# Another order of bank pairs, with accumulating transfers, in the last five stages of a hybrid trunk kernel on one Trainium2 core

## The chip, the core and the metric

One core of one Trainium2 chip runs the whole kernel. The core has a matrix engine (TensorE, "PE" in the profile), a vector engine (VectorE, "DVE"), a scalar engine (ScalarE, "ACT"), a general engine (GpSimd, "POOL") and a queue engine (SyncE, "SP"). TensorE writes its sums into PSUM banks; VectorE and ScalarE read them out. All other data lies in SBUF, and DMA transfers carry it to and from device memory. Each engine works through its own list of instructions in order, and semaphores tie the lists together. The metric is the time of one execution on the device, in microseconds (us); lower is better.

## What is computed

One layer of a streaming model, for a prompt of 1024 rows and eight samples of 16 rows, 1152 rows in all, which the kernel takes as one width of 1152 (two halves of 576, each of two pieces of 288):

```python
h = rms_norm(x, norm_g) * (1 + scale) + shift          # from c @ w_ada
z = h @ w_in    # attention q | k | v | gate | SSD gate | SSD x/B/C | dt | two merge gates
a = (attention over a band of chunks, gated) @ w_att_proj
s = (SSD scan of x/B/C, gated, group norm)   @ w_ssd_proj
y = (sigmoid(g_a) * a + sigmoid(g_s) * s) @ w_out
out = x + mod_gate * y
```

All matrices of 1024 columns that stand at the end (merge gates, attention projection, SSD projection over 2048 rows, output projection) are multiplied as float32 values split into a high and a low fp16 part, with three of the four partial products.

## The kernel before

**The last five stages.** After attention and the SSD scan the program has five dense stages: the merge gates (their last four pairs; eight plain ones go before), the attention projection (`att_dense`), the first half of the SSD projection (`ssd_dense(0)`), its second half (`ssd_dense(1)`) and the output projection (`out_dense`). Each stage has four "quads", 20 in all. A quad computes two column blocks (o = 0, 1) of 128 for both halves (t = 0, 1) of the width, by a scheme of Winograd's kind: seven products in place of eight, on sums and differences of operand blocks and of weight blocks. One product is 24 matmuls of 128x288: four blocks of the inner dimension, two PSUM banks (the two pieces of 288), three fp16 terms (lines 854, 855, 856).

**Banks.** A product goes to a pair of PSUM banks. The pool `s` has one pair of banks; the pools `g` and `d` have three single banks each. In `quad_dense` a pair is two banks of one pool, and the names are `fore` (from `s` in one quad, from `d` in the next), `side` (from `g`) and `lone` (from `s` or `d`, whichever `fore` isn't). Products 0, 5, 6 and 3 are summed one onto the other in `fore`, products 4 and 2 in `side`, product 1 stands alone in `lone`; between two products of one pair the running sum must be read out. The order of a quad is 0, 4, 5, 1, 6, 2, 3. The first quad of each stage (`wide`) interleaves products 0, 4 and 1 by inner block, because its operands are still being made, and reads `fore` out once more before product 3 (`u3`), which then has a pair of its own.

**Reading out.** `kept` copies a pair by ScalarE (line 873, two instructions of 288 columns) or, in the second SSD half, adds it by VectorE onto the first half's result, called the base (line 869). `joined` adds a pair by VectorE onto a copy that was kept (line 879). Product 3's sum goes straight to the stage's own last step (lines 2293, 2309, 2325 by stage).

**Operands.** The right side of a stage is cut into pieces by `pieces`: ScalarE and VectorE make a high part (`halved`, lines 2173 and 2175) and a low part, and differences (lines 2184 to 2187). For the attention projection they come from `att_d`, for the SSD projection from `y_d` times a row of token scales `yb` (lines 2250, 2256, 2261), for the output projection from the merged result below. Line 686 (ScalarE) squares pieces for a running check of magnitudes. Weights are loaded 512 KB at a time (`in_quad_dram`), and split by lines 694 (ScalarE) and 695 (VectorE).

**The merge.** `att_dense` multiplies its result by its gate (line 2293) and stores it in device memory as `att_o` (line 2296, issued by POOL, 16 stores of 128x576). `ssd_dense(0)` stores `acc_d` (lines 2309, 2310). `ssd_dense(1)` loads `acc_d`, the gates and `att_o` again (tiles `acc`, `gs`, `att` of 128x1152, by SP), adds the products onto `acc`, multiplies by the gate (line 2329, 128x576) and adds that onto the `att` tile by VectorE (line 2330, 128x576, 16 times). The `att` tiles, two for each pair, then go through `pieces` into the output projection.

**What sets the order.** Python generators emit the work of each stage in program order (`run`), with `urgent` and `paced` side jobs that give way to each other by an estimated clock: `pause(t)` holds a job until t ns of that clock have gone by, `stored` gives a buffer back 9000 ns after its store. SBUF buffers come from an arena (`walloc`, `alloc`); a job that finds no room waits. Then the class `Order` sorts the instructions of each engine anew: a list scheduler with a cost and a margin for each engine (`SAFE`) and a reach of `AHEAD` instructions. Its result is the order of the queues; what an instruction waits for on the chip is still set by semaphores. `token_sums` (line 1364) sums squares over the columns by three matmuls, after `pause(4500)`; `mod_gate` makes the gate of the output from `c` (matmuls on lines 1077 and 1083, ScalarE on 2357) beside the attention projection. After the last quad a check of all magnitudes (`verdict`, lines 2379 to 2393) decides whether a general kernel must run in place of this one.

## Time and profile before

| | |
|---|---|
| median of three runs | 1721.31 us (1721.12 to 1727.28) |
| the profiled execution | 1722.93 us, span 1721.0 us |
| TensorE matmul | busy 1677.3 us (97%) |
| VectorE | busy 1378.6 us (80%) |
| ScalarE | busy 1061.5 us (62%) |
| POOL | busy 391.5 us (23%) |
| the five stages | from about 1275 us to the end, 20 quads |

The span is the time from the first instruction to the last on the core; the execution's own time is 1.9 us longer. TensorE's matmuls are pipelined: one is shown as 0.28 us long, while they start 0.12 us apart, so that "busy" doesn't mean that none can be put in. The number in square brackets in a timeline is how long the engine was idle just before that instruction, with what ended it.

### The profile page before, as it was taken

Reading aid. Unit: us, or ns where it says so; the run is one execution under the profiler, and the core shown is the slowest. Engines: PE = TensorE matmul, PEld = TensorE weight load, DVE = VectorE, ACT = ScalarE, POOL = GpSimd, SP = SyncE. Lnnn points to the kernel's source line nnn. Section 1 sums busy time; section 2 is a strip of 40 time slices with the busy share of each in tenths; the row PEclk is TensorE's granted clock in tenths of the full one; section 3 lists DMA queues with packets and bytes.
Section 4 is the critical chain, followed back from the end, with each engine's and each line's share of the span. In section 5 each row is a group of like instructions: output and inputs, shape, how many; then the busy total and the mean of one; then the engine's idle time right before and its main releaser. Section 6 shows DMA issues by size and latency. Waiting matters only on the chain.

```text
span 1721.0 us, 36673 instructions
## 1 busy us (share of the span) xinstructions
PE 1677.3 (97%) x14265; PEld 1122.4 (65%) x14265; DVE 1378.6 (80%) x2546; ACT 1061.5 (62%) x2130; POOL 391.5 (23%) x640
## 2 busy tenths in 40 slices
PE   7999999999999999999999999999999999999998
PEld 3556565556565556666666666666667677777776
DVE  6458767878777888989988989996898487878963
ACT  8766556566565567456655756666388575775550
POOL 0134233135133101322321333242231011110000
PEclk9999999999999999999999999999999999999999
DMA  9248789797988688686858767878658786777651
GB/s 383 83 120 212 169 227 228 169 230 189 210 227 189 168 190 228 184 220 199 196 182 271 231 184 242 238 217 272 226 166 294 266 292 207 254 284 259 221 194 58
DMA packets 299105, 369.16 MB, mean 214 GB/s; under 512 B 211676, under 2 KB 213096, under 8 KB 298920
## 3 DMA queue, kind: packets, MB, share of 16 engines
q1 hardware_dynamic: 281896, 307.65, 63.7%
q0 software_dynamic: 17024, 59.06, 9.4%
q8 instruction: 114, 1.87, 0.5%
q14 instruction: 71, 0.58, 0.1%
HBM read 244.08 MB, written 74.06 MB: 185 GB/s over the span
## 4 chain that ended last, share of the span: by engine, by line
PE 51%; DVE 18%; DMA 11%; ACT 11%; issue 7%; POOL 1%; SPq 1%; DVEq 0%; ACTq 0%; POOLq 0%
PE d L945 6%; PE d L948 6%; PE d L946 6%; PE d L998 5%; PE d L1000 5%; PE d L999 5%; ACT arena L686 3%; PE g L1604 2%; DVE arena L2175 2%; DMA arena<-in_quad_dram 2%; DMA arena<-acs_d 2%; DVE arena L695 2%; DVE arena L1802 2%; ACT arena L1988 1%; DMA arena<-sum_d 1%
## 5 line engine op out<-in xcount | busy, mean ns | idle before, releaser
L945 PE MATMUL d<-arena 128*128 128x384 f16 x1320 | 431.0, 327 | 1.4 <-ACT arena L1779 1.4
L948 PE MATMUL d<-arena 128*128 128x384 f16 x1320 | 430.3, 326 | 0.6 <-DVE arena L695 0.6
L946 PE MATMUL d<-arena 128*128 128x384 f16 x1320 | 430.3, 326 | 0.0
L686 ACT ACTIVATE arena<-arena 128x1024 bf16<-128x1024 f32 (+4 forms) x217 | 199.3, 918 | 141.9 <-DMA arena<-in_wall_dram 96.4
L695 DVE SCALAR_TENSOR_TENSOR arena<-arena 128x1024 f16<-128x1024 f32 (+2 forms) x157 | 181.7, 1165 | 42.4 <-ACT arena L694 42.2
L694 ACT ACTIVATE arena<-arena 128x1024 f16<-128x1024 f32 (+2 forms) x157 | 155.1, 994 | 66.5 <-DMA arena<-sum_d 33.1
L945 PEld LDWEIGHTS <-arena 128*128 128x128 f16 x1320 | 129.2, 98 | 90.2 <-issue 13.3
L998 PE MATMUL d<-arena 128*128 128x384 f16 (+1 forms) x568 | 186.8, 329 | 0.0
L1000 PE MATMUL d<-arena 128*128 128x384 f16 (+1 forms) x568 | 186.1, 328 | 0.0
L999 PE MATMUL d<-arena 128*128 128x384 f16 (+1 forms) x568 | 186.1, 328 | 0.0
L948 PEld LDWEIGHTS <-arena 128*128 128x128 f16 x1320 | 129.1, 98 | 86.3 <-DVE arena L695 1.0
L946 PEld LDWEIGHTS <-arena 128*128 128x128 f16 x1320 | 129.2, 98 | 78.5 <-issue 1.6
L1544 ACT ACTIVATE arena<-arena 128x640 f32<-128x640 f32 (+4 forms) x144 | 100.8, 701 | 63.5 <-DVE arena L1547 63.1
L855 PEld LDWEIGHTS <-arena 128*128 128x128 f16 x1120 | 109.7, 98 | 43.9 <-issue 16.3
L854 PE MATMUL d<-arena 128*128 128x288 f16 x440 | 126.3, 287 | 3.7 <-ACT arena L873 3.2
L856 PEld LDWEIGHTS <-arena 128*128 128x128 f16 x1120 | 109.8, 98 | 30.5 <-issue 2.7
L854 PEld LDWEIGHTS <-arena 128*128 128x128 f16 x1120 | 110.0, 98 | 29.5 <-issue 1.7
L855 PE MATMUL d<-arena 128*128 128x288 f16 x440 | 126.2, 287 | 1.1 <-DVE arena L2175 1.1
L856 PE MATMUL d<-arena 128*128 128x288 f16 x440 | 126.1, 287 | 0.0
L854 PE MATMUL s<-arena 128*128 128x288 f16 x360 | 102.9, 286 | 6.5 <-ACT arena L873 3.9
L1802 DVE SCALAR_TENSOR_TENSOR arena<-arena 128x1176 f32<-128x1176 f32 x72 | 103.2, 1434 | 5.5 <-ACT arena L1799 3.8
L2175 DVE SCALAR_TENSOR_TENSOR arena<-arena 128x1152 f16<-128x1152 f32 (+1 forms) x72 | 87.4, 1219 | 21.9 <-ACT arena L2173 21.7
(278 smaller groups left out, 3565.0 us busy)
## 6 DMA issues: line engine op xcount, KB each, us to landing
arena<-in_quad_dram SPq DMA_DIRECT2D x80, 512.0 KB, 5.7
arena<-in_wall_dram SPq DMA_DIRECT2D x77, 512.0 KB, 5.2
sum_d<-arena POOLq DMA_DIRECT2D x40, 512.0 KB, 4.7
arena<-sum_d SPq DMA_DIRECT2D x40, 512.0 KB, 4.8
arena<-acs_d SPq DMA_DIRECT2D x32, 576.0 KB, 5.8
arena<-in_kc_dram SPq DMA_DIRECT2D x64, 256.0 KB, 4.6
arena<-in_vc_dram SPq DMA_DIRECT2D x64, 256.0 KB, 2.9
arena<-in_wada_dram SPq DMA_DIRECT2D x24, 512.0 KB, 10.2
```

The costliest lines, as they stand in the source:

```text
L686: keep(nc.scalar.activation(junk[:, :n], x, AF.Square, scale=scale * n ** -0.5, accum_out=sums[:, c:c + 1]))
L694: keep(nc.scalar.activation(hi, x, AF.Copy, scale=scale))
L695: keep(nc.vector.scalar_tensor_tensor(lo, x, scale, hi, ALU.mult, ALU.subtract))
L854: nc.tensor.matmul(ps, wh, xh[:, c], start=first and k == 0, stop=False, skip_group_check=not first)
L855: nc.tensor.matmul(ps, wh, xl[:, c], start=False, stop=False, skip_group_check=not first)
L856: nc.tensor.matmul(ps, wl, xh[:, c], start=False, stop=k == 3, skip_group_check=not first)
L945: nc.tensor.matmul(ps, hi.r[:, wc], kh.r[:, tok], start=k == 0, stop=False)
L946: nc.tensor.matmul(ps, hi.r[:, wc], kl.r[:, tok], start=False, stop=False)
L948: nc.tensor.matmul(ps, lo.r[:, wc], kh.r[:, tok], start=False, stop=k == nk - 1)
L998: nc.tensor.matmul(ps, kh.r[:, tok], wh, start=k == 0, stop=False)
L999: nc.tensor.matmul(ps, kh.r[:, tok], wl, start=False, stop=False)
L1000: nc.tensor.matmul(ps, kl.r[:, tok], wh, start=False, stop=k == KT - 1)
```

## The change

1. **Order of products.** A quad now runs 0, 4, then product 3 of the quad before (`rest`, held in `pending` and emitted by `flush`), 5, 1, 2, 6. In a `wide` quad the product held over is emitted after the first inner block. `lone` is a fourth pair made of one bank of pool `d` and one of pool `g`. The extra read-out of `fore` in wide quads (`u3`) is gone.
2. **Quick read-outs.** Instructions that read PSUM in these stages are marked; `Order` puts them 300 places ahead and plans a margin of 200 ns for them.
3. **Weights.** The buffers of split weights are taken part by part and given back after the product that uses them last (`w_used`); splitting can go up to two quads ahead (`w_next`).
4. **The merge.** For three of the four pairs in the second SSD half, `att_o` is added by 12 accumulating transfers from device memory into the `acc` tile in SBUF (line 2364 of the new kernel, issued by POOL, 128x576 each). The 12 VectorE adds and six of the eight loads of `att_o` are gone; the pieces of these pairs come from `acc`, after a `pause(9000)`. The last pair still loads `att_o` (`att_last`) and adds by VectorE.
5. **Side jobs.** Loads of the merge tiles follow each half of a pair, `token_sums` pauses for 12000, and `mod_gate` runs at the start of the gates stage.

```diff
+    FAST = 300
+    SAFE_FAST = 200.0
...
+            u["fast"] = u["ins"][0].name in self.fast
+            u["at"] = u["i"] + self.FILL * (u["ins"][0].name in self.fill) - self.FAST * u["fast"]
...
-                    m = self.SAFE_DMA if v["dma"] else self.SAFE[u["eng"]]
+                    m = self.SAFE_DMA if v["dma"] else self.SAFE_FAST if u["fast"] else self.SAFE[u["eng"]]
...
+    pending = []
+
+    def flush():
+        while pending:
+            yield from pending.pop()()
+
+    def quick(x):
+        fast.add(x.ins.name)
+        return x
...
-            return [psd.tile([P, HC], F32, tag="d", name=nm("d")) for _ in range(2)]
-
-        fore = bank(2 if odd else 0)
-        side = bank(1)
+            if n == 2:
+                return [psd.tile([P, HC], F32, tag="d", name=nm("d")) for _ in range(2)]
+            return [psd.tile([P, HC], F32, tag="d", name=nm("d")), pg(HC)]
...
+                if k == 0:
+                    yield from flush()
             begun.update((0, 4, 1))
         yield from product(0, fore)
         p1 = yield from kept(fore, 0, 0)
         yield from product(4, side)
         p5 = yield from kept(side, 1, 1)
+        yield from flush()
+        w_next(i)
         yield from product(5, fore, first=False)
+        w_used(i, 3, 4)
         u2 = yield from kept(fore, 0, 1)
         w_next(i)
-        if not wide:
-            lone = bank(0 if odd else 2)
+        lone = lone or bank(3)
         yield from product(1, lone)
+        w_used(i, 0, 1)
         yield from joined(0, 0, p1, lone)
         w_next(i)
-        if wide:
-            yield from product(2, side, first=False)
+        yield from product(2, side, first=False)
+        yield from joined(0, 1, u2, side)
         yield from product(6, fore, first=False)
...
-        if wide:
-            lone = bank(0 if odd else 2)
-            yield from product(3, lone)
-            yield from joined(1, 0, u3, lone)
-        else:
+        def rest():
             yield from product(3, fore, first=False)
+            w_used(i, 2)
             yield from evict(1, 0, [(g * HC, HC, ps) for g, ps in enumerate(fore)], None) or ()
-        w_done(i)
+
+        pending.append(rest)
...
-                yield from pause(4500)
+                yield from pause(12000)
...
-                m = yield from taken("att", c + o)
+                m = a if c < 6 else (yield from taken("att", o))
...
-                nc.vector.tensor_tensor(m.ap[:, tok], m.ap[:, tok], a.ap[:, tok], ALU.add)
+                if c < 6:
+                    nc.gpsimd.dma_start(a.ap[:, tok], att_o[c + o][:, tok], accum_op=ALU.add)
+                else:
+                    nc.vector.tensor_tensor(m.ap[:, tok], m.ap[:, tok], a.ap[:, tok], ALU.add)
...
-                        urgent.append(pieces(tiles["att"][c], m, out_ops, 0.5 * SM / (SA * SW)))
+                        def last(c=c, m=m):
+                            if c < 6:
+                                yield from pause(9000)
+                            yield from pieces(tiles["acc"][c] if c < 6 else tiles["att"][0], m, out_ops, 0.5 * SM / (SA * SW))
+                        urgent.append(last())
...
-        yield from ready(lambda: len(att_ops) >= 1)
+        yield from ready(lambda: ssd_all[NPAIR])
...
-    items.append((att_dense(), [tile_loads(4, ("ga", gate_d, 0)), ssd_prep(), mod_gate()], [], 0.5))
+    items.append((gates_dense(), [mod_gate(), h_pieces(), att_prep()], [], 0.5))
+    items.append((att_dense(), [tile_loads(4, ("ga", gate_d, 0)), ssd_prep()], [], 0.5))
```

**How it moves instructions.** The first place is VectorE's list in the second quad of the second SSD half. Before, `d_17644`, `d_17645` are the `fore` banks, `g_17646`, `g_17647` the `side` banks, and `s_17749` the `lone` pair:

```order
L869 TENSOR_TENSOR arena<-arena,d_17644 128x288
L869 TENSOR_TENSOR arena<-arena,d_17645 128x288
L879 TENSOR_TENSOR arena<-arena,s_17749 128x288 x2
L879 TENSOR_TENSOR arena<-arena,g_17646 128x288
L2175 SCALAR_TENSOR_TENSOR arena<-arena 128x1152
L2329 SCALAR_TENSOR_TENSOR arena<-arena 128x576
L879 TENSOR_TENSOR arena<-arena,g_17647 128x288
L2330 TENSOR_TENSOR arena<-arena 128x576
L879 TENSOR_TENSOR arena<-arena,d_17644 128x288
L879 TENSOR_TENSOR arena<-arena,d_17645 128x288
L2329 SCALAR_TENSOR_TENSOR arena<-arena 128x576 x2
L2330 TENSOR_TENSOR arena<-arena 128x576 x2
```

In the new kernel the same stretch reads as follows; `d_17602`, `d_17603` are the `fore` banks, `g_17604`, `g_17605` the `side` banks, `d_17722` with `g_17723` the fourth pair, and L901, L2362, L2200 and L2211 are the lines that were L879, L2329, L2175 and L2186:

```order
L901 TENSOR_TENSOR arena<-arena,d_17722 128x288
L901 TENSOR_TENSOR arena<-arena,g_17723 128x288
L698 SCALAR_TENSOR_TENSOR arena<-arena 128x512
L2362 SCALAR_TENSOR_TENSOR arena<-arena 128x576
L901 TENSOR_TENSOR arena<-arena,g_17604 128x288
L901 TENSOR_TENSOR arena<-arena,g_17605 128x288
L2362 SCALAR_TENSOR_TENSOR arena<-arena 128x576
L2200 SCALAR_TENSOR_TENSOR arena<-arena 128x1152
L901 TENSOR_TENSOR arena<-arena,d_17602 128x288
L901 TENSOR_TENSOR arena<-arena,d_17603 128x288
L2211 SCALAR_TENSOR_TENSOR arena<-arena 128x576
L2362 SCALAR_TENSOR_TENSOR arena<-arena 128x576
```

The adds L2330 that followed each gate multiplication are gone from the list, and the two read-outs of a pair stand side by side.

The second place is the end of POOL's list; before:

```order
L2152 DMA gate_d<-arena 128x576 x16
L2296 DMA att_o<-arena 128x576 x16
L2310 DMA acc_d<-arena 128x576 x16
L4159 TENSOR_LOAD again
L4160 COMPARE_AND_BRANCH
```

and in the new kernel:

```order
L2177 DMA gate_d<-arena 128x576 x15
L2329 DMA att_o<-arena 128x576 x16
L2343 DMA acc_d<-arena 128x576 x16
L2364 DMA arena<-att_o 128x576 x12
L4201 TENSOR_LOAD again
L4202 COMPARE_AND_BRANCH
```

The 12 accumulating transfers come behind all stores of POOL's queue, and only the final load of the check's answer comes behind them.

The third place is ScalarE's list ahead of the first quad of the gates, whose banks `s_14627`, `g_14628`, `g_14629` it reads out; before:

```order
L1894 ACTIVATE arena<-d_14594 128x384
L686 ACTIVATE arena<-arena 128x576
L2173 ACTIVATE arena<-arena 128x1152
L686 ACTIVATE arena<-arena 128x576 x3
L694 ACTIVATE arena<-arena 128x1024
L2173 ACTIVATE arena<-arena 128x1152
L686 ACTIVATE arena<-arena 128x1024
L873 ACTIVATE arena<-s_14627 128x288 x2
L873 ACTIVATE arena<-g_14628 128x288
L873 ACTIVATE arena<-g_14629 128x288
```

and in the new kernel, where the banks are `s_14646`, `g_14647`, `g_14648`, and L1919, L689, L697, L2198, L895 are the lines that were L1894, L686, L694, L2173, L873:

```order
L1919 ACTIVATE arena<-d_14601 128x384
L689 ACTIVATE arena<-arena 128x576 x2
L2397 ACTIVATE arena<-g_14629 128x512
L1391 ACTIVATE arena<-g_14656 96x384
L697 ACTIVATE arena<-arena 128x1024
L689 ACTIVATE arena<-arena 128x576 x2
L2198 ACTIVATE arena<-arena 128x1152
L689 ACTIVATE arena<-arena 128x576 x2
L697 ACTIVATE arena<-arena 128x512
L2198 ACTIVATE arena<-arena 128x1152
L895 ACTIVATE arena<-s_14646 128x288 x2
L895 ACTIVATE arena<-g_14647 128x288
```

The read-out of the output gate's matmuls (L2397, from `mod_gate`) and of the token sums (L1391) now stand ahead of this quad's first read-outs.

116 lines of the change are left out of this document (65 added, 51 removed).

## The prediction

> **What bounds the kernel now.** First the page, for the share of each engine and the matrix engine's clock over the span:
>
> ```profile
> span 1721.0 us, 36673 instructions
> PE 1677.3 (97%) x14265; PEld 1122.4 (65%) x14265; DVE 1378.6 (80%) x2546; ACT 1061.5 (62%) x2130; POOL 391.5 (23%) x640
> ```
>
> TensorE bounds the kernel, and no matmul is taken away. What a change of this kind can win is TensorE's stalls. So the second view is what TensorE waited for, over the stretch of the quads (1270 to 1721):
>
> ```profile
> PE s L854 <- ACT arena L873: 3.9, 3, 2.3
> PE d L854 <- ACT arena L873: 3.2, 3, 1.7
> PE g L854 <- ACT arena L873: 2.4, 1, 2.4
> PE s L854 <- DVE arena L879: 1.3, 1, 1.3
> PE g L854 <- DVE arena L869: 1.2, 1, 1.2
> PE g L855 <- DVE arena L2175: 1.2, 1, 1.2
> PE d L855 <- DVE arena L2175: 1.1, 1, 1.1
> PE s L854 <- DVE arena L869: 0.7, 1, 0.7
> PE g L2393 <- DVE arena L2391: 0.6, 1, 0.6
> PE s L854 <- ACT arena L2309: 0.5, 1, 0.5
> PE d L854 <- DVE arena L879: 0.4, 1, 0.4
> PE d L854 <- ACT arena L2173: 0.2, 1, 0.2
> ```
>
> Each row gives the total, the count and the longest. All but four rows are the first matmul of a product waiting for a bank that ScalarE or VectorE has still to read: 3.9 + 3.2 + 2.4 + 1.3 + 1.2 + 0.7 + 0.5 + 0.4 = 13.6 us in 12 waits. Three waits, 1.2 + 1.1 + 0.2 = 2.5 us, are for operands. The check's 0.6 us stays. Over the whole run the same view has one more row that the change touches:
>
> ```profile
> PE g L1364 <- DVE arena L2123: 2.4, 2, 1.4
> ```
>
> Third, the timeline at the longest of these waits, and at the slowest stretch behind it:
>
> ```profile
> 1374.23 0.28 PE L854 MATMUL g<-arena 128*128 128x288 f16 x1 [2.35 <-ACT arena L873]
> 1374.35 0.28 PE L855 MATMUL g<-arena 128*128 128x288 f16 x1
> 1374.47 0.28 PE L856 MATMUL g<-arena 128*128 128x288 f16 x1
> 1634.52 0.28 PE L854 MATMUL s<-arena 128*128 128x288 f16 x1 [2.26 <-ACT arena L873]
> 1640.69 0.44 PE L856 MATMUL g<-arena 128*128 128x288 f16 x1
> 1640.93 0.44 PE L854 MATMUL g<-arena 128*128 128x288 f16 x1
> ```
>
> Matmuls start 0.12 us apart (1374.23, 1374.35, 1374.47), so a product of 24 lasts 24 x 0.1225 = 2.94 us. At 1640.69 they are 0.24 us apart: half the pace. The windows there show the clock that was granted, as the last number but two:
>
> ```profile
> 1638.00:1642.00 4.00, 2.40 (x13) 1.52 (x13) 3.97 (x7) 3.97 (x8) 0.00 (x0) 0.76 0.41 125
> 1642.00:1646.00 4.00, 4.00 (x29) 2.90 (x28) 4.00 (x4) 3.23 (x5) 0.00 (x0) 0.81 0.77 244
> ```
>
> 0.24 and 0.19 of 4 us each are lost to the clock: 1.7 us. An idle figure understates a wait: it counts from the end of a 0.28 us matmul, where the next would have started 0.12 after it, so each costs 0.16 us more. The 12 bank waits cost 13.6 + 12 x 0.16 = 15.5 us; the operands 2.5 + 3 x 0.16 = 3.0, with the clock 4.7; the token sums 2.4. That is 22.6 us that the change could win.
>
> **Part one: the order of products.** In the narrow quads before, 0, 4, 5, 1, 6, 2, 3, the pair `fore` gets products 0, 5, 6, 3 with one other product between each two: three times, 2.94 us in which the sum must be read. After, 0, 4, 3', 5, 1, 2, 6 (3' from the quad before), there are two products between each two uses: 5.9 us. What a read-out takes:
>
> ```profile
> L873 ACT ACTIVATE arena<-s x42: 387/402/428, 1286.0 to 1680.9; 128x288 f32<-128x288 f32 x42
> L879 DVE TENSOR_TENSOR arena<-arena,d x50: 443/446/455, 1290.5 to 1707.1; 128x288 f32<-128x288 f32 x50
> ```
>
> Two of either are 0.8 to 0.9 us, so one product suffices unless the reading engine is late by more than 2 us; two products forgive 5 us. Over 15 narrow quads 45 tight places go. In the wide quads the old order has 6 in all. In the new one about 25 remain, all in wide quads or where stages meet. I price them as those of before: 15.5 us over 51 places is 0.30 each; 25 x 0.30 = 7.6 us stay, 7.9 are won. That is the cautious value: walking the engines' lists at each wait of before with the durations above, I find only about 3 us of stalls left, which would win 12.4. I take the count, since a place-by-place walk sees only the waits that exist now. The low end is nothing: the waits are for engines that are late, and the longest has such a cause:
>
> ```profile
> 1371.26 1.42 DVE L2261 SCALAR_TENSOR_TENSOR arena<-arena 128x1152 f32<-128x1152 f32 x1 [5.58 <-DMA arena<-yb]
> 1372.72 1.16 ACT L2173 ACTIVATE arena<-arena 128x1152 f16<-128x1152 f32 x1 [8.51 <-DVE arena L2261]
> ```
>
> VectorE sat 5.58 us at a load of `yb`, ScalarE 8.51 us behind VectorE, and TensorE 2.35 us behind ScalarE's copy. Two products of cover take 2.94 us off such a wait, all of this one.
>
> At the very end the new order loses: the last quad's product 3 has no next quad to be held into, so it follows product 6 with nothing between, and waits for that pair's read-out. Two adds of 0.45 us, less the 0.16 that the pipeline hides, are 0.75 us lost; nothing covers it.
>
> **Part two: quick read-outs and removed copies.** Ten copies on ScalarE (5 wide quads, 2 each, 0.40 us: 4.0) and ten adds on VectorE (0.446: 4.5) go. I cost them at nothing: they lie beside matmuls. The read-outs that are put ahead push weight splitting back; the weights' cover is the earlier freeing of their buffers. No wait for a weight buffer stands in the view of waits, so this too is nothing, and at worst the 0.30 a place already charged.
>
> **Part three: the accumulating transfers.** VectorE's load in the second SSD half, and what it removes:
>
> ```profile
> 1440.00:1520.00 80.00, 77.57 (x631) 61.42 (x629) 72.61 (x91) 61.11 (x115) 8.11 (x15) 1.00 0.69 226
> 1520.00:1618.00 98.00, 94.50 (x767) 74.81 (x765) 85.01 (x129) 56.58 (x96) 2.70 (x5) 1.00 0.73 258
> 1618.00:1646.00 28.00, 23.21 (x173) 17.41 (x173) 25.59 (x37) 17.05 (x28) 0.00 (x0) 0.94 0.70 243
> L2330 DVE TENSOR_TENSOR arena<-arena x16: 747/750/758, 1553.3 to 1631.4; 128x576 f32<-128x576 f32 x16
> ACT arena L686: 14.1, 8
> ```
>
> The columns are matmul, weight load, VectorE, ScalarE and POOL. The last two windows are this half and its passage into the output projection: VectorE is 87% and 91% busy, and there it is what makes operands late. Twelve adds of 0.750 us are 9.0 us of it. ScalarE waited 14.1 us in 8 times for those adds; it will now wait for transfers. In the stretch from 1618 on, TensorE was idle for 28 - 23.2 = 4.8 us: the bank wait of 2.26 at 1634.52, which part one counts, and the 2.5 for operands. In the new order there are 99 matmuls (12.1 us) between the last product of the half and the first use of its last pieces, and the chain between is 5 to 7 us of instructions of the sizes above. So of the 4.7 us (operands and slow clock) I take 4.3 as won; the low end is 0, if VectorE's list stays as late.
>
> What the trace before does not show is an accumulating transfer. The nearest rows are plain ones of 288 KB by POOL, and loads by SP:
>
> ```profile
> att_o<-arena POOLq DMA_DIRECT2D x16, 288.0 KB, 4.6
> acc_d<-arena POOLq DMA_DIRECT2D x16, 288.0 KB, 5.1
> DMA to landing us min/median/max: 2.4/5.1/7.5
> arena<-att_o SPq DMA_DIRECT2D x8, 576.0 KB, 8.0
> arena<-yb SPq DMA_DIRECT2D x4, 576.0 KB, 10.5
> ```
>
> The third row belongs to the second (the stores on line 2310). The bounds are 2.4 and 10.5 us; I take 5.1, since the size and the queue are those of these stores, and POOL is idle there (2.70 of 98 us). From the end of a product to the reader of its transfer there are by the new lists about 72 matmuls, 8.8 us; the read-out and the gate multiplication ahead of the transfer are some 2.5, so a landing under 6.3 us costs nothing. At 5.1 it is free; behind it the reader would be the first instruction of `pieces`, and all of VectorE's or ScalarE's list behind that. The Trainium skill (DMA: Bandwidth & Descriptors, "Anatomy of one DMA — SWDGE (gpsimd) path") gives 2.0 us plus bytes / 436e3 for such a transfer, an estimate of 2.7 us here; the stores' 4.6 and 5.1 disagree, and the sum is the same by either.
>
> **Part four: the side jobs.** `token_sums` waits twice for VectorE's sum, 2.4 us. A pause of 12000 for 4500 moves these matmuls 7.5 us of work further on: won, 2.4. The output gate's matmuls are moved, not added.
>
> **Sum.** 7.9 + 4.3 + 2.4 - 0.75 = 13.9 us. The profiled execution of 1722.93 becomes 1709.0; against the median of 1721.31 that is 1707.4, and I say 1707. A measurement of this kernel can tell about 0.5% (8.6 us) from no change, so faster begins at 1712.7 and slower at 1729.9.
>
> **The rivals.** *The waits move (20%).* ScalarE and VectorE work in order, and a list that stands 5.58 us at `yb`, whose load took 10.5 us, takes every read-out behind it along; the 300 places and the 200 ns margin plan that a read-out comes early, not that the engine is free. Then of the 15.5 us nothing is won, of the 4.7 about 3, and with the 2.4 and the 0.75 lost the gain is about 5: 1716. For it: the wide quads keep their tight places, and the longest wait above came from an engine held up elsewhere. Against it: the 45 narrow places go whatever the reason.
>
> *The accumulating transfers land late (10%).* This is the side that is slower. If they take as long as the `yb` load, 10.5 us, each of the 12 holds its reader 10.5 - 6.3 = 4.2 us: 50 us. VectorE's idle time there, 13.0 + 2.4, and the 9.0 freed, absorb 24.4; the other 26 lengthen the stage, less what is won elsewhere (4 of the 7.9, the 2.4, less 0.75: 5.6): 1721 + 26 - 6 = 1741. It decides from a landing of 6.3 + 24.4 / 12 = 8.3 us on, and the sign turns at 8.3 + 5.6 / 12 = 8.8. For it: a transfer that reads, adds and writes does more than a store, the DMA share there is 0.73, and the `att_o` loads took 8.0. Against it: those carry twice the bytes. The Trainium skill (SBUF — State Buffer, "Who interferes with whom") speaks for it: GpSimd prepares its transfers through ports shared with VectorE and stops while VectorE holds them in some modes. By it landings would be longest where VectorE is busiest. The stores of `acc_d`, most of them in the window from 1440 with VectorE 91% busy, took 7.5 us at the longest, under the 8.3, and that is why the chance is small.
>
> *All of it is won (8%).* If only the 3 us of the walk remain, with part three whole: 12.4 + 4.7 + 2.4 - 0.75 = 18.8, to 1702; if the new places cost nothing either, 1699.
>
> **How the numbers follow.** The forecast (a gain of 9 to 17) has 62%, more won 8%, the moved waits 20%, late transfers 10%. The first two are faster, 70%. The moved waits and a fifth of the late transfers (a landing up to 8.3 + (5.6 + 8.6) / 12 = 9.5 us) are the same, 22%; 8% are slower. The range takes in the walk's end and the moved waits: 1700 to 1719. Below it lies some 3%, above it 12%.
>
> **What would show it.** Right: in the quads' stretch TensorE's waits for read-outs fall from 13.6 us in 12 to some 6, and sit in wide quads; the row L1364 is gone; VectorE has under 78 us in the second SSD half; the transfers land in 4 to 6 us; no stretch with a clock under 0.9 behind 1618; one new wait of half a microsecond or more at the last product. Wrong: waits of readers for the accumulating transfers of several us each; or the same sum of waits of TensorE under other lines, in narrow quads too.

## The result

The changed kernel is slower: a median of 1737.5 us (1734.8 to 1749.3, six runs) against 1722.4 for the kernel before, a ratio of 1.0086 with an interval of 1.006 to 1.0112. The forecast was 1707. The profiled execution took 1738.76 us. The page of the changed kernel begins:

```profile
span 1737.0 us, 36678 instructions
PE 1685.0 (97%) x14265; PEld 1126.0 (65%) x14265; DVE 1367.6 (79%) x2527; ACT 1060.9 (61%) x2123; POOL 386.4 (22%) x652
```

VectorE has 11.0 us less to do, as the change says (1378.6 before), and the span is 16.0 us longer. What TensorE waited for in the quads of the changed kernel (total, count, longest; L876 and L877 are matmuls, L901 `joined`, L891 the add onto the base, L895 the copy, L2198 and L2200 the operands):

```profile
PE d L876 <- DVE arena L901: 11.9, 5, 5.8
PE s L876 <- DVE arena L891: 1.6, 1, 1.6
PE s L876 <- ACT arena L2198: 1.5, 1, 1.5
PE g L877 <- DVE arena L2200: 1.2, 1, 1.2
PE s L876 <- DVE arena L901: 1.0, 1, 1.0
PE d L876 <- DVE arena L891: 0.8, 1, 0.8
PE g L876 <- DVE arena L901: 0.8, 1, 0.8
PE s L877 <- DVE arena L2200: 0.5, 1, 0.5
PE d L877 <- DVE arena L2200: 0.3, 1, 0.3
PE s L876 <- ACT arena L895: 0.2, 1, 0.2
```

The waits for ScalarE's copies, 9.5 us before, are nearly gone (0.2). In their place five waits for VectorE's `joined` hold 11.9 us, one of them 5.8. The new order alone doesn't explain the first: the kernels below that share it have between 0.2 and 7.1 us of waits for these copies. And not all of the second comes from one cause: two of the five waits, 2.44 us at 1389.92 and 2.51 at 1545.76, lie ahead of the first accumulating transfer (1558.6), so no such transfer can be their cause; the first stands behind a load of `yb` that took 11.85 us, as the longest wait of before did.

To see where the 16 us lie, I cut each trace at the starts of matmuls: the first matmul of 128x288, then every 672nd (four quads), then the last; "ahead" is what lies before, "end" what lies behind. These are start times in the traces, in us; the stage of a product that is held over shifts by one product.

| kernel | ahead | gates | attention | SSD 1 | SSD 2 | output | end |
|---|---|---|---|---|---|---|---|
| before | 1275.5 | 85.5 | 90.5 | 87.0 | 85.1 | 89.2 | 8.2 |
| changed | 1285.7 | 84.0 | 86.5 | 89.6 | 96.4 | 84.7 | 10.1 |

Ahead of the quads 10.2 us were added. 5.6 of them are the output gate's matmuls, which moved from the attention stage to here: the nine traces with these matmuls in the attention stage, that of before among them, show 90.0 to 90.7 there (mean 90.3), the five with them moved 83.1 to 86.5 (mean 84.6). Another 3.0 us were already there at the 5171st matmul of 128x384 (1193.9 us before, 1196.9 after). In that first part the traces of all the kernels below stand between 1.4 and 14.1 us behind the one of before, though TensorE's list is nearly the same up to there. Two traces of one and the same kernel lie almost 6 us apart there. I don't explain this spread; because of it each verdict below goes by ratios of many runs, and the traces serve only for stretches behind it. The second SSD half and the output projection, 174.3 us together before, are 181.1 now. The end is 1.9 longer.

**The chain behind the longest wait.** The timeline of the changed kernel at the passage into the output projection, from the last accumulating transfer on (POOL, ScalarE, VectorE, TensorE):

```profile
1629.22 0.85 POOL L2364 DMA_DIRECT2D arena<-att_o  x1 [10.20 <-PE g L878]
1636.26 0.68 ACT L689 ACTIVATE arena<-arena 128x576 bf16<-128x576 f32 x1 [3.47 <-DMA arena<-att_o]
1638.56 1.72 ACT L2198 ACTIVATE arena<-arena 128x1152 f16<-128x1152 f32 x2
1639.73 1.36 DVE L2200 SCALAR_TENSOR_TENSOR arena<-arena 128x1152 f16<-128x1152 f32 x1 [3.39 <-ACT arena L2198]
1641.01 0.81 DVE L901 TENSOR_TENSOR arena<-arena,d 128x288 f32<-128x288 f32 x2
1641.51 0.40 PE L876 MATMUL d<-arena 128*128 128x288 f16 x1 [5.80 <-DVE arena L901]
```

The transfer was issued at 1629.22; ScalarE was ready for the first square of the piece (L689) 3.57 us later, at 1632.79, and could begin it at 1636.26, after 3.47 us of waiting. Three squares and the high part (L2198) follow. VectorE's low part (L2200) stood 3.39 us for that, and behind it in VectorE's list stood the read-out (L901) that TensorE needed. TensorE was idle for 5.80 us. The transfers as a group, in the view of line 2364:

```profile
L2364 POOL DMA_DIRECT2D arena<-att_o x12: 837/846/909, 1558.6 to 1629.2; - x12
ACT arena L689: 13.3, 5
DVE arena L2209: 4.3, 1
DMA to landing us min/median/max: 4.2/7.1/8.4
```

They land after 7.1 us at the median, not 5.1, and readers waited 17.6 us for them. In the six waits the reader was ready 3.6 to 5.6 us after the issue of its transfer, not 6.3.

**The clock.** Windows of the changed kernel behind its longest waits; the last number but two is the granted clock:

```profile
1263.00:1267.00 4.00, 3.83 (x16) 2.62 (x17) 4.00 (x5) 4.00 (x7) 1.08 (x2) 0.56 0.52 86
1267.00:1271.00 4.00, 4.00 (x20) 1.73 (x18) 4.00 (x8) 1.07 (x2) 0.54 (x1) 0.58 0.94 363
1389.00:1393.00 4.00, 3.08 (x14) 1.93 (x14) 4.00 (x9) 3.94 (x10) 0.54 (x1) 0.60 0.12 16
1545.00:1549.00 4.00, 3.24 (x18) 2.23 (x18) 3.66 (x7) 1.81 (x4) 0.54 (x1) 0.73 1.00 348
1640.00:1644.00 4.00, 2.49 (x11) 1.60 (x11) 4.00 (x7) 2.13 (x5) 0.00 (x0) 0.50 0.36 140
1644.00:1648.00 4.00, 4.00 (x28) 2.84 (x27) 4.00 (x7) 1.02 (x1) 0.00 (x0) 0.78 0.00 0
```

The shortfall from 1.00 over these windows is 1.76 + 1.68 + 1.60 + 1.08 + 2.00 + 0.88 = 9.0 us, against 1.7 before. Cut at the edges of the slow stretches it is 10.2, of which 1.3 fall into the waits themselves and cost nothing, so 8.9 are left. Four waits of TensorE (2.47, 2.44, 2.51 and 5.80 us, 13.2 together) came just ahead of these stretches or ran into them, so a long wait cost about two thirds more than its own length.

### The profile page after: what moved, and what is told of

The parts are those of the page before. It is cut to its first block, busy times and chain, and to the rows that moved or that the text cites. A ratio compares the mean times of both kernels' runs of the same rounds, so it can differ in the third digit from the quotient of the medians.

```text
span 1737.0 us, 36678 instructions
## 1 busy us (share of the span) xinstructions
PE 1685.0 (97%) x14265; PEld 1126.0 (65%) x14265; DVE 1367.6 (79%) x2527; ACT 1060.9 (61%) x2123; POOL 386.4 (22%) x652
## 4 chain that ended last, share of the span: by engine, by line
PE 55%; issue 16%; DVE 11%; DMA 8%; ACT 7%; POOL 2%; SPq 0%; POOLq 0%; DVEq 0%; ACTq 0%
PE d L970 7%; PE d L973 7%; PE d L971 7%; PE d L1023 5%; PE d L1025 5%; PE d L1024 5%; PE g L1629 2%; DMA arena<-acs_d 2%; ACT arena L689 1%; DVE arena L1827 1%; DMA arena<-att_o 1%; PE s L1676 1%; PE g L1676 1%; DMA arena<-in_wall_dram 1%; DMA arena<-arena 1%
## 5 line engine op out<-in xcount | busy, mean ns | idle before, releaser
L689 ACT ACTIVATE arena<-arena 128x1024 bf16<-128x1024 f32 (+4 forms) x217 | 199.2, 918 | 133.0 <-DMA arena<-in_wall_dram 88.5
L698 DVE SCALAR_TENSOR_TENSOR arena<-arena 128x1024 f16<-128x1024 f32 (+2 forms) x157 | 181.7, 1164 | 59.2 <-ACT arena L697 58.5
L697 ACT ACTIVATE arena<-arena 128x1024 f16<-128x1024 f32 (+2 forms) x157 | 155.3, 993 | 82.1 <-DMA arena<-sum_d 44.7
L877 PEld LDWEIGHTS <-arena 128*128 128x128 f16 x1120 | 110.3, 99 | 48.4 <-issue 20.3
L876 PEld LDWEIGHTS <-arena 128*128 128x128 f16 x1120 | 110.4, 99 | 30.0 <-issue 1.5
L876 PE MATMUL d<-arena 128*128 128x288 f16 x400 | 116.4, 291 | 12.7 <-DVE arena L901 11.9
L877 PE MATMUL d<-arena 128*128 128x288 f16 x400 | 116.4, 291 | 0.3 <-DVE arena L2200 0.3
L878 PE MATMUL d<-arena 128*128 128x288 f16 x400 | 116.4, 291 | 0.0
L877 PE MATMUL g<-arena 128*128 128x288 f16 x400 | 114.8, 287 | 1.2 <-DVE arena L2200 1.2
L876 PE MATMUL g<-arena 128*128 128x288 f16 x400 | 114.9, 287 | 0.8 <-DVE arena L901 0.8
L878 PE MATMUL g<-arena 128*128 128x288 f16 x400 | 114.7, 287 | 0.0
```

Source lines behind the costliest of these rows:

```text
L689: keep(nc.scalar.activation(junk[:, :n], x, AF.Square, scale=scale * n ** -0.5, accum_out=sums[:, c:c + 1]))
L697: keep(nc.scalar.activation(hi, x, AF.Copy, scale=scale))
L698: keep(nc.vector.scalar_tensor_tensor(lo, x, scale, hi, ALU.mult, ALU.subtract))
L876: nc.tensor.matmul(ps, wh, xh[:, c], start=first and k == 0, stop=False, skip_group_check=not first)
L877: nc.tensor.matmul(ps, wh, xl[:, c], start=False, stop=False, skip_group_check=not first)
L878: nc.tensor.matmul(ps, wl, xh[:, c], start=False, stop=k == 3, skip_group_check=not first)
```

## The experiments

The parts are taken apart by undoing them in the changed kernel, and by putting one alone into the kernel before. Theory T is the chain above. Rival O says that the new order of read-outs makes VectorE late by itself. Theory M concerns the moved output gate. Beside these experiments the kernel before had medians from 1725 to 1727, with single runs 1% apart; what counts is the ratio of each kernel to the runs of before on the same chip.

### The sum by VectorE again

```diff
-                if c < 6:
-                    nc.gpsimd.dma_start(a.ap[:, tok], att_o[c + o][:, tok], accum_op=ALU.add)
-                else:
-                    nc.vector.tensor_tensor(m.ap[:, tok], m.ap[:, tok], a.ap[:, tok], ALU.add)
+                nc.vector.tensor_tensor(m.ap[:, tok], m.ap[:, tok], a.ap[:, tok], ALU.add)
...
-                            if c < 6:
-                                yield from pause(9000)
...
```

> The new kernel with attention's result added by VectorE again for all four pairs (loads of att_o by SP as before); everything else as changed. Theory T (ScalarE's squares wait for the accumulating transfers, VectorE's next operand waits for ScalarE, and the read-outs of PSUM stand behind it): the second SSD half and the output projection, 181.1 us together in the new kernel against 174.3 before, come back to about 172, and the time falls from 1737 to about 1727. Rival O (the new order of products and read-outs makes VectorE's list late by itself): 9 us of VectorE come on top, the two stages stay at 181 or grow, and the time is 1735 to 1742.

Ratio 0.9992 (0.9966 to 1.0018), median 1724.1 us. The two stages took 82.3 + 88.1 = 170.4 us, the end 6.5. This is theory T's size. Rival O, which had 181 or more, is out as the cause of this loss. The two stages in windows, first of this kernel and then of the changed one:

```profile
1547.10:1629.40 82.30, 82.30 (x674) 65.74 (x672) 73.58 (x119) 40.15 (x64) 1.08 (x2) 1.00 0.74 256
1629.40:1717.50 88.10, 84.75 (x677) 66.56 (x676) 54.84 (x102) 33.28 (x61) 0.00 (x0) 0.98 0.42 143
```

```profile
1545.80:1642.20 96.40, 85.39 (x673) 66.54 (x673) 70.15 (x112) 45.47 (x72) 11.32 (x14) 0.97 0.82 247
1642.20:1726.90 84.70, 84.52 (x676) 66.66 (x675) 51.94 (x99) 29.40 (x53) 0.00 (x0) 0.98 0.36 121
```

With VectorE's adds TensorE has no idle time at all in the second SSD half (82.30 of 82.30), though VectorE is busy for 89% of it. Without them VectorE is busy for 73%, and TensorE loses 11 us. Busy time of VectorE was not the limit.

### The accumulating transfers alone, in the kernel before

```diff
-                nc.vector.tensor_tensor(m.ap[:, tok], m.ap[:, tok], a.ap[:, tok], ALU.add)
+                if c < 6:
+                    nc.gpsimd.dma_start(a.ap[:, tok], att_o[c + o][:, tok], accum_op=ALU.add)
+                else:
+                    nc.vector.tensor_tensor(m.ap[:, tok], m.ap[:, tok], a.ap[:, tok], ALU.add)
...
+                            if c < 6:
+                                yield from pause(9000)
```

> The kernel before with the 12 accumulating transfers and the late loads of att_o for the last pair alone; old order of products, old margins, old place of the side jobs. Theory T: the transfers land about 7 us after their issue here too, ScalarE waits for them some 10 us in all, and the time grows from 1722 by 6 to 10 us, to about 1730. Rival O: the transfers are harmless with the old order, VectorE has 9 us less to do, and the time is 1719 to 1723.

Ratio 1.0107 (1.0049 to 1.0166; four runs), median 1741.5; the profiled execution, at 1732.3 us, is the fastest of the four. So with the old order, where a product is the only cover, the transfers cost about as much or more. Line 2339 of this kernel is the transfer:

```profile
ACT arena L686: 24.6, 8
DVE arena L2184: 2.3, 1
DMA to landing us min/median/max: 4.2/6.7/8.1
```

ScalarE's squares (L686) waited 24.6 us, where some 10 were expected; the two stages took 96.1 + 85.6 = 181.7 us, and the end 12.9.

### The output gate back in the attention stage

```diff
-        yield from ready(lambda: ssd_all[NPAIR])
+        yield from ready(lambda: len(att_ops) >= 1)
...
-    items.append((gates_dense(), [mod_gate(), h_pieces(), att_prep()], [], 0.5))
+    items.append((gates_dense(), [h_pieces(), att_prep()], [], 0.5))
```

> The new kernel with the output gate's matmuls back beside the attention projection. Theory M (TensorE waits 2.5 us for ScalarE's copy of these matmuls' result ahead of the first quad, and runs some 4 us at half clock behind it): the 2.7 us of wait and about 2 us of slow clock go, the time falls from 1737 to about 1732. Rival: the wait and the slow clock are only moved to where the matmuls now lie, and the time stays at 1737 within 2.

Ratio 1.0048 (1.0023 to 1.0073), median 1732.6, where the changed kernel had 1.0086. The wait is seen in the timeline of the changed kernel:

```profile
1263.17 1.61 PE L1108 MATMUL g<-arena 128*128 128x9 f32 x8 [2.47 <-ACT arena L2397]
```

ScalarE's copy L2397 stood behind squares of other pieces, and the clock was at 0.56 and 0.58 in the two windows behind it (above), a shortfall of 3.4 us. In the old place a wait remains ahead of the same matmuls (1.9 us for `joined`), without a slow clock. In the traces the stretch from the 5171st matmul of 128x384 to the first quad is 79.0 to 83.5 us long with the gate in the old place (nine traces, mean 80.0) and 86.9 to 88.8 with it moved (five, mean 88.2); less the 5.6 us that go from the attention stage, the move costs 2.6 us. The ratios differ by 0.4%, with intervals that overlap (1.006 to 1.0112 for the changed kernel). In the kernels without transfers, below, the same move makes 0.3% and 0.0% (0.9992 against 0.9966 and 0.9989). So the wait and the 2.6 us are seen in the traces, and a loss of time from them is not shown beyond the noise.

### Nobody reads the transfers

```diff
-                    nc.gpsimd.dma_start(a.ap[:, tok], att_o[c + o][:, tok], accum_op=ALU.add)
+                    nc.gpsimd.dma_start(g.ap[:, tok], att_o[c + o][:, tok], accum_op=ALU.add)
...
-                            if c < 6:
-                                yield from pause(9000)
```

> The new kernel with the 12 accumulating transfers aimed at the spent gate tile, which nobody reads: same traffic, same issues by POOL, but no reader waits for them (attention's part is left out of three of the four pairs, and the pieces of these pairs are made without the pause of 9000). Theory T: what costs is the reader's wait; the second SSD half and the output projection fall from 181 to 170 or less, the time to about 1725. Rival D (the transfers cost by their traffic, in the way of the weight loads, or by POOL): the two stages stay near 181 and the time near 1735.

Ratio 1.0021 (0.9997 to 1.0045), median 1731.0. The two stages took 88.2 + 84.5 = 172.7, near the 170.4 of VectorE's adds, with the same transfers in flight (median landing 6.8 us). So against the kernel with VectorE's adds the waiting of readers carries most of the loss there, 8.4 of 10.7 us. The edit does two things more: the pause of 9000 goes, and the gate tile is given back later (`stored`). The time fell less than expected, which leaves something for rival D, the traffic; the next run shows more of it.

### The same transfers without the sum

```diff
-                    nc.gpsimd.dma_start(g.ap[:, tok], att_o[c + o][:, tok], accum_op=ALU.add)
+                    nc.gpsimd.dma_start(g.ap[:, tok], att_o[c + o][:, tok])
```

> As the run in which nobody reads the 12 transfers, but as plain transfers of the same size from device memory into the spent gate tile, without the sum (attention's part is left out of three of four pairs here too). It measures the price of the sum itself. If adding is what makes a transfer slow: landing falls from a median of 6.8 us to 4 to 5, POOL's issue from 0.85 to 0.54, and POOL's last drain from 1.7 us to 0.7, so 1 to 3 us less at the close. If the direction (into SBUF, by POOL) is what costs: landing and close stay as they are with the sum.

Ratio 1.0003 (0.9974 to 1.0032), median 1726.8. POOL's issue and the landing in this kernel:

```profile
L2364 POOL DMA_DIRECT2D arena<-att_o x12: 536/536/551, 1562.1 to 1620.8; - x12
DMA to landing us min/median/max: 3.0/4.0/6.2
```

A plain transfer of this size, by the same engine, lands after 4.0 us; with the sum it is 6.8 in the run before this one and 7.1 in the changed kernel, and the issue 0.85 for 0.54. That is the price the trace before did not hold. The close went the other way than expected: POOL's last drain stayed at 1.7 us, so it isn't the sum that lengthens it (see the next run).

This kernel and the one before it have the same list of instructions on every engine, and differ in the sum alone. Yet the two stages took 83.8 + 83.0 = 166.8 us here and 172.7 there. TensorE waited 0.2 us in them here and 4.6 there, and ScalarE 11.6 and 17.9 us for the loads of weight sums (`sum_d`). So a transfer that adds seems to cost by its traffic too, up to 5.9 us, with nobody reading it. That rests on one trace of each, and the two ratios don't part them.

### Only the first pair by transfers

```diff
-                m = a if c < 6 else (yield from taken("att", o))
+                m = a if c < 2 else (yield from taken("att", c - 2 + o))
...
-                if c < 6:
+                if c < 2:
                     nc.gpsimd.dma_start(a.ap[:, tok], att_o[c + o][:, tok], accum_op=ALU.add)
```

> The new kernel with the old place of the output gate's matmuls, and only the first of the pairs by accumulating transfers (4 of the 12); the other three by VectorE. With 12 the second SSD half and the output projection took 178.6 us together, with none 170.7. If each waiting reader costs its part: about a third of the 7.9, so 173 to 174. At the close, if the longer end is a fixed cost of having such transfers at all, POOL's last drain stays at 1.7 us; if it goes by their number, it falls to about 1.05. Ratio 0.998 to 1.002, between those of none and of 12 (0.9966 and 1.0048).

Ratio 1.0007 (0.9983 to 1.0031), between those of none and of twelve, as expected; the interval doesn't part it from none. But in the trace the two stages took 91.2 + 90.8 = 182.0 us, as long as with twelve, where a third was expected. The first long wait on VectorE is at a transfer; a wait of TensorE of 3.2 us comes some 19 us later:

```profile
1573.21 0.76 DVE L2210 TENSOR_TENSOR arena<-arena 128x576 f32<-128x576 f32 x1 [4.80 <-DMA arena<-att_o]
1585.32 0.68 ACT L689 ACTIVATE arena<-arena 128x576 bf16<-128x576 f32 x1 [3.11 <-DVE arena L901]
1589.17 1.36 DVE L2200 SCALAR_TENSOR_TENSOR arena<-arena 128x1152 f16<-128x1152 f32 x1 [3.94 <-ACT arena L2198]
```

ScalarE came late to a piece of the second pair, which VectorE adds, VectorE's low part stood 3.94 us for ScalarE's high part, and TensorE 3.2 us for the read-out behind it. It is the same chain as in the result, and a transfer stands at its head here too: from 1573.21, when VectorE came free of it, to 1585.24, when it released ScalarE, VectorE worked without a gap. The profile's own chain, followed back, goes from there to a transfer that landed after 8.09 us (its first piece, and the last ones ahead of TensorE):

```profile
1565.00 8.09 DMA arena<-att_o
1588.08 1.06 ACT arena L2198
1589.17 1.36 DVE arena L2200
1592.15 0.45 DVE arena L891
```

So one late transfer is enough for such a wait, and in this trace the loss doesn't go by their number. Transfers are not the only thing that makes a piece late: TensorE's wait of 3.53 us for an operand at 1639.89 in this kernel comes far behind the last of the four, issued at 1577.0, and a kernel without any, below, has one of 2.9 us. These two stages also differ by some us from one trace to the next: 168.6 to 173.1 in the six traces with the new order and without transfers, of which 170.7 and 173.1 are of the same kernel. POOL's last drain by the number of added transfers, of the changed kernel (12), of this one (4) and of the kernel before (none):

```profile
L4337 POOLq DRAIN  x3: 40/107/1707, 1734.4 to 1736.7; - x3
```

```profile
L4337 POOLq DRAIN  x3: 40/107/1053, 1724.9 to 1726.6; - x3
```

```profile
L4295 POOLq DRAIN  x3: 40/107/727, 1719.4 to 1720.8; - x3
```

(1707 - 727) / 12 = 82 ns and (1053 - 727) / 4 = 82 ns: each of the added transfers lengthens POOL's last drain by 0.08 us, with or without a sum. The 184 transfers that POOL issues in the kernel before can't have that price, since all of its drain is 0.727 us; what sets the added ones apart is not shown.

### A later reader

```diff
                             if c < 6:
-                                yield from pause(9000)
+                                yield from pause(14000)
```

> The new kernel with the pause ahead of the accumulated pieces 14000 for 9000. Theory T: the readers come later in ScalarE's list, its waits for the transfers fall from 13.3 us to under 7, second SSD half and output projection fall from 181 to 174 to 177, the time to about 1732. Rival (a later reader makes the output projection's operands late instead): the sum of the two stages stays at 179 to 183, with TensorE's waits moved into the output projection.

Ratio 1.0040 (1.0011 to 1.0068), median 1733.5. The squares' wait for the transfers, 13.3 us in the changed kernel, is now:

```profile
ACT arena L689: 6.4, 5
```

The two stages took 89.9 + 84.5 = 174.4 us; the landing was the same (7.0). Halving the readers' wait (17.6 to 8.6 us with VectorE's) gave back 6.7 of the 10.7 us that the transfers cost there. This is theory T's forecast, and the rival's (operands late in the output projection) didn't come.

### Without the transfers and without the moved gate

Both edits of the first and third experiment in the changed kernel, on two chips:

> The new kernel with both the VectorE adds and the old place of the output gate's matmuls: order of products, fourth pair, quick read-outs, weights and the longer pause of the token sums stay. If the two undone parts carry the whole loss and add up: 1274 us ahead of the quads (as in the two runs with the old place), second SSD half and output projection 170.4 (as in the run with VectorE's adds), so about 7 us under the kernel before, ratio 0.994 to 0.998. Rival (the order of products wins nothing, what it takes at one place it gives back at another): ratio 0.998 to 1.002.

> The kernel with the order, the fourth pair, the quick read-outs and the token sums' pause, without accumulating transfers and with the output gate's matmuls in their old place, once more on the same chip as the next. If it beats the kernel before: ratio 0.994 to 0.999, interval under 1.000. If the first result was chance: 0.999 to 1.002.

Ratios 0.9966 (0.9942 to 0.9989) and 0.9989 (0.9962 to 1.0015).

### The mark on read-outs, and the order alone

```diff
     def quick(x):
-        fast.add(x.ins.name)
         return x
```

> The run above without the mark on read-outs (no places ahead, the old margin). If the quick read-outs carry the gain of the new order: back to 1.000 and TensorE's waits for read-outs in the quads grow by 5 us or more. If the order of products and the fourth pair carry it: within 0.2% of the run above.

Ratio 0.9997 (0.997 to 1.0023). TensorE's waits for read-outs in the quads are 7.9 us here and 6.7 and 6.2 in the two traces with the mark, so the 5 us or more didn't come. Then, with the token sums' pause at 4500 again as well, on two chips:

> The order of products, the fourth pair and the handling of weights alone: no accumulating transfers, no moved output gate, no mark, token sums after 4500. Against the run before it this takes back only the token sums' pause: two waits of 2.4 us together return ahead of the quads, so 0.1 to 0.15% slower than that run; a difference over 0.4% would say that the pause moves more than its own waits.

> The order, the fourth pair and the weights alone, beside the run above on one chip. If the mark on read-outs and the longer pause win what the prediction took for the token sums (2.4 us): 0.1 to 0.2% above the run above. If they win nothing: the same ratio within 0.2% either way.

Ratios 0.9972 (0.9947 to 0.9997) and 0.9970 (0.9948 to 0.9992), medians 1721.3 and 1721.6. The order of products with the fourth pair and the weights alone is the version that beats both kernels, the one of before by about 0.3% or 5 us. The mark and the longer pause add nothing that these runs can tell: with them 0.9966 and 0.9989, with the pause alone 0.9997, without both 0.9972 and 0.9970, with intervals that overlap.

TensorE's waits in the quads of the kernel with the order alone (first run; its lines are one less than the changed kernel's, and L1101 is a matmul of the output gate):

```profile
PE s L875 <- ACT arena L894: 4.1, 4, 1.6
PE g L1101 <- DVE arena L900: 1.9, 1, 1.9
PE d L875 <- ACT arena L2197: 1.5, 1, 1.5
PE s L875 <- DVE arena L890: 1.5, 1, 1.5
PE d L876 <- DVE arena L2199: 1.1, 1, 1.1
PE s L876 <- DVE arena L2199: 1.0, 2, 0.7
PE g L875 <- ACT arena L894: 0.8, 1, 0.8
PE d L875 <- DVE arena L900: 0.4, 2, 0.2
```

Waits of matmul products for read-outs are 4.1 + 1.5 + 0.8 + 0.4 = 6.8 us (8.5 in the second run), against 13.6 before.

All stretches together, cut as above (us):

| kernel | ratio | SSD 2 + output | end |
|---|---|---|---|
| before | 1 | 174.3 | 8.2 |
| changed | 1.0086 | 181.1 | 10.1 |
| transfers alone in the kernel before | 1.0107 | 181.7 | 12.9 |
| gate back (12 transfers) | 1.0048 | 178.6 | 9.0 |
| first pair only (4 transfers), gate back | 1.0007 | 182.0 | 6.7 |
| later reader | 1.0040 | 174.4 | 8.6 |
| nobody reads | 1.0021 | 172.7 | 8.4 |
| plain, nobody reads | 1.0003 | 166.8 | 8.8 |
| VectorE's adds | 0.9992 | 170.4 | 6.5 |
| VectorE's adds, gate back | 0.9966, 0.9989 | 170.7, 173.1 | 6.3, 6.1 |
| the same without the mark | 0.9997 | 168.6 | 6.5 |
| order alone | 0.9972, 0.9970 | 169.8, 169.6 | 6.5, 6.6 |

## Why the prediction was wrong

The ratios add up within their noise: the order gives -0.3%, the transfers +0.6 to +1.1% (1.0048 against 0.9966 and 0.9989, 1.0086 against 0.9992, and 1.0107 alone), the moved gate 0.0 to +0.4%; together +0.3 to +1.2%, and 0.86% was measured. Each is known to some 0.25% only, so this is agreement and no proof. That the transfers are the main part is shown: without them the loss is gone (0.9992), and alone they make one (1.0107).

**Part three failed, at "I take 5.1".** The landing was 7.1 us at the median. The direction was clear from the bounds (2.4 to 10.5, and "a transfer that reads, adds and writes does more than a store" stood under the rival), but I took the row of the same size and queue. The price of the sum is about 3 us a transfer, by the pair 4.0 and 6.8. The Trainium skill's fit that I quoted (DMA: Bandwidth & Descriptors, "Anatomy of one DMA — SWDGE (gpsimd) path"), an estimate of 2.7 us, is under both.

**And at "a landing under 6.3 us costs nothing".** In the six waits of the changed kernel the reader was ready 3.6 to 5.6 us after the issue. At the 5.1 us that I took, five of the six would still have waited (one of them by 0.1 us), and where the gate is back and the median landing was 6.3 us, readers waited 9.6 us. So the cover was mis-sized as much as the landing, and 5.1 was not free. Which of its two terms was off, the 8.8 or the 2.5, stays open.

**And at the point from which it decides.** By the rival's arithmetic a landing of 7.1 is past 6.3, where it begins to cost, and short of 8.3, where I let VectorE's idle time run out, so it still would have been free. That absorption was the error. Idle time of an engine can't be drawn on when its list is in order: what stands behind a waiting operand includes the read-out that TensorE needs next. The first reader was moreover on ScalarE, whose wait I did not put ahead of VectorE's. TensorE lost 11 us of the second SSD half while VectorE was busy for 73% of it. So the rival "the accumulating transfers land late" is what happened, from a lower point on than I set, and at 10% it was too small; its 1741 was close to the 1737.5 for a reason that was only half right.

**Part four failed for the output gate.** "Moved, not added" took the cost as nothing. The wait for ScalarE's copy ahead of the gates and the half clock behind it cost 2.6 us in the traces; the ratios put it anywhere from 0.0 to 0.4%. I had quoted that very row of ScalarE's list as a place where something moved, and did not ask what TensorE does until that copy is done. The token sums' wait of 2.4 us did go from the changed kernel's trace, but the time of the kernels with and without the longer pause shows no gain.

**Part one was right in kind and too large in size.** Read-out waits went from 13.6 to 6.8 and 8.5 us in the kernels with the order alone; the forecast was some 6. That is 5 to 7 us against the forecast's 7.9, of which 1.9 come back as the wait of the output gate's first matmul. The 4.3 us for operands and slow clock at the passage were not won as such: waits for operands are 3.6 us in that kernel, 2.5 before. (That kernel keeps VectorE's adds, so it doesn't test the part of the 4.3 that was to come from their removal.) What was measured for all of it is 0.3%, 5 us, against 11.45 in the sum (7.9 + 4.3 - 0.75).

**The end was wrong in sign.** The last product does wait for VectorE's add (0.2 us in the kernel with the order alone), but the end fell from 8.2 to 6.5 us, since the check's last sums now stand ahead of the last product. With 12 added transfers it is 8.4 to 12.9: 1.0 us of it is POOL's longer drain, and the rest lies on POOL's queue between the branch and that drain.

**Part two held.** The removed copies and adds, and the mark on read-outs, changed nothing that can be told.

What stays open: the spread of 1.4 to 14.1 us ahead of 1200 us, and what POOL waits for at its close in the kernels with 12 added transfers (in all six its queue stands 1.9 to 3.4 us between two semaphores there; one more transfer of instructions falls in that stretch, which is a hint and no proof), and how much of the loss is the traffic of the transfers and not the wait for them.

## What to carry to other kernels

Work that is taken from a busy engine and given to a transfer must be priced by the latency of its first reader, and by everything that stands behind that reader in an in-order list, not by the busy time that it frees. A transfer that adds is not a transfer that stores: measure one before planning 12 of them. When a matmul is moved "for nothing", look up who reads its result, and what stands ahead of that reader.

## What the runs showed of the hardware

- An accumulating transfer of 288 KB from device memory into SBUF, issued by POOL, lands after 6.3 to 7.6 us at the median (six kernels) where the plain one takes 4.0, and POOL is held 0.85 us for its issue instead of 0.54.
- Each of the added transfers lengthens POOL's drain at the end of the kernel by 82 ns, accumulating or plain (0.727 us without them, 1.053 with 4, 1.707 with 12). The 184 transfers that the kernel before has already don't each cost that: its whole drain is 0.727 us.
- In the changed kernel every wait of TensorE of 2.4 us or more in this stretch had a lower granted clock at its end or soon after it (0.50 to 0.78 in windows of 4 us), while the kernel before had one of 2.35 us without, and one of 2.26 us with two more waits soon after it. From 1240 us on TensorE's waits are 22.3 us, against 17.7 before; the lost clock, up to the last product, is 8.9 us against 1.5.
- The length of a wait alone doesn't decide: the transfers alone in the kernel before have a wait of 2.52 us (1371.23) with the clock at 1.00 behind it. In all 14 traces the slow stretches up to the last product are 3.41 or 6.83 us long at 0.50, and within one trace their starts are multiples of 3.41 us apart. Cut into such windows (from 60 us on), the traces have 34 full-clock windows with a slow one behind them, and in 31 of these TensorE was idle for 1.95 us or more (in the other three for 1.25, 1.79 and 1.89); in the 6703 full-clock windows without a slow one behind them it was idle for 1.96 us at most. So a wait that falls across two windows, as the 2.35 us of before does (1.96 us in the first), can pass without a slow stretch.
- The Trainium skill (TensorE: Matmul & The Clock Gate, "What's actually happening") has the clock fall after an idle window of some 3.4 us. The 3.41 us agree; but some 1.95 us of idle time in a window sufficed here, and waits of 2.44, 2.47 and 2.51 us, so the measurement differs.
